# Weight sums of a Strassen-type layer: two groups made anew instead of stored, operand splits ahead of the sink, and the sums of the later products spread over the columns of path A

## The chip, the cores and the metric

The kernel runs on one core of a Trainium2 chip. The metric is the device time of one execution in microseconds; the time before is the median of three runs, and a separate execution was recorded by the hardware profiler. All numbers are float32, multiplied as fp32r (a rounded form that the matrix engine takes) in three passes, high by high, high by low and low by high. TensorE appears as PE (matmuls) and PEld (weight loads), VectorE as DVE, ScalarE as ACT, GpSimd as POOL, SyncE as SP, and SP's queue of transfers as SPq.

## What is computed

One layer of a recurrent mixer over 2048 prompt tokens and 64 sample tokens, with 1024 features. Cut to what matters here:

```python
h = rms_norm(x, g_pre)
vA, bA, cA, zA, q, f, iv, zB, gA, gB = split_cols(h @ w_in)      # ten products, 1024 x 1024 each
conv = causal_conv3([conv_hist, cA * vA], conv_w)
yA = (silu(zA) * bA * conv) @ w_a_out                            # path A
S_new, o = hgrn2_scan(S0, silu(q) * scale, 1 - fg, iv, log(fg))  # path B: 8 heads, chunks of 64 tokens
yB = (rms(o) * g_onorm * silu(zB)) @ w_b_out
merged = sigmoid(gA) * yA + sigmoid(gB) * yB
x = x + rms_norm(merged @ w_o, g_post)
x = x + (p @ w_ple_proj) * sigmoid(rms_norm(x, g_ple) @ w_ple_gate)
```

The kernel names the products `VA, CA, ZA, BA` (path A), `FF0, ZB0, GB...` (path B and the gates), `W_A = w_a_out`, `W_B = w_b_out`, `W_O = w_o` and `W_G = w_ple_gate`.

## The kernel before

**Tiling.** The 2112 tokens are three blocks (0, 1, 2) of 704, features on the partitions. Each matmul takes a 128x128 weight block and half a block of tokens, 352 columns. Weights come from memory in tiles of 128x512 (`raw`, 256 KB, 5 buffers); `split_w` casts each on ACT to `hi` and subtracts on DVE to get `lo`.

**Seven products in place of eight.** `sgroup` (lines 345 to 400) takes two 128-column groups of two products with all 1024 input features as a 2x2 block product and does it with seven half-size products of the Strassen-Winograd kind (lines 380 to 382: high-high, high-low, low-high). This needs four sums of weight quarters, `S1` to `S4` (`total`, line 303), their splits, and sums of the results on DVE (lines 394 to 426: `hf` tiles hold products copied out of the accumulators; the `sink` of each caller writes the outputs). Every product is 12 matmuls, and a group of 7 products 84.

**What is stored.** In block 0, `combined` makes S1 to S4 and the lows of all quarters and stores them in memory (`keep_sum`; `S<-s`, `low<-lo`). Blocks 1 and 2 load sums and lows back (`kept_w`; `raw<-S`, and `s<-low` or `lo<-low`), so that DVE need not make them. The low of a kept quarter goes by turns into an `s` tile (3 of 7; 3 buffers, which the sums use too) or a `lo` tile (`low_tile`). Two groups are not made in block 0, because their products go another way there: the first of head 0 of path B (`FF0`) and the gate columns 6 and 7 (`GB`). `combined` makes their sums when it meets them first, in block 1, and POOL stores sums (line 284) and lows (line 231) for block 2.

**W_A, W_B, W_O and W_G in the same form.** `prepare_sums` makes their sums ahead with loads on POOL's queue (`r<-w_blk`, line 328), sums on DVE (line 358) and stores on POOL (339 sums, 335 lows). It is a generator; hooks between products, or steps of `merge`, call for its next part. `in_turn` (line 486) then goes product by product over all four column groups `g`: at product `n` of group `g` it runs twelve matmuls (lines 513 to 515), the sink (for W_A and W_B: line 419 and line 1171, in the last product, n = 6), and `prepare(i + 1, g)`, which splits the operand of the next product (`operand_of`, DVE line 194). In block 0, W_A and W_B go through `merge` as plain products, and only W_O goes in turn, with its sums made in `merge`.

**Order.** For each block: path B (8 heads, with chunk attention in between), path A (`path_a`, 8 columns j, each a `VA/CA` group, the convolution, and a `ZA/BA` group), W_A, W_B, W_O, the norms, the gates of the next block. Each engine goes through its own list of instructions; the program's order with priorities fixes it. POOL's and SP's transfers are issued in such lists as well, so a transfer that waits holds back those behind it.

Of the kernel before, what the change touches and what calls it, by code (L numbers as in the profile page):

```python
# [20 lines left out]
KB = D // P  # L21
# [67 lines left out]
def hybrid_step(  # L89
# [155 lines left out]
    last, hooks, copies, adds = [None], [], [None], [None]  # L245
# [35 lines left out]
    def keep_sum(name, i1, s, queue):  # L281

        sums.setdefault(i1, {})[name] = dram.tile([P, 4, P], F32, tag=f"{name}_{i1}", name=nm(name), bufs=1)
        queue.dma_start(sums[i1][name], s)
        return split_w(s, (i1, name), queue)
# [8 lines left out]
    def combined(i1, i2, first):  # L294

        queue = SP if first else G
        with tc.high_priority():
            if not first and i1 in sums:
                return {n: kept_w(i1, i2, n) for _, n, _, _, _ in PRODUCTS}
            a11, a21, a22, a12 = (load_raw(w_blk[i, h]) for i, h in ((i1, 0), (i2, 0), (i2, 1), (i1, 1)))  # L300
            out = dict(A11=split_w(a11, (i1, 0), queue))

            def total(name, x, y, op):
                s = sum_tile()
                V.tensor_tensor(s, x, y, op)
                out[name] = keep_sum(name, i1, s, queue)
                return s

            total("S3", a11, a21, ALU.subtract)
            s1 = total("S1", a21, a22, ALU.add)  # L310
            s2 = total("S2", s1, a11, ALU.subtract)
            out["A12"] = split_w(a12, (i1, 1), queue)
            out["A22"] = split_w(a22, (i2, 1), queue)
            total("S4", a12, s2, ALU.subtract)
            return out
# [112 lines left out]
    def plain_group(i1, i2, hs, sink, raws=None, between=None):  # L428


        w, ps = {}, {}

        def split_of(c, h):
            key = ((i1, i2)[c], h)
            raw = raws[c, h] if raws else load_raw(w_blk[key])
            with nullcontext() if raws else tc.high_priority():
                w[c, h] = split_w(raw, key)

        for c, h in ((0, 0), (1, 0)) if between else ((0, 0), (0, 1), (1, 0), (1, 1)):
            with behind_all(() if between else summed[2 + c]):  # L440
                split_of(c, h)

        def add(c, ks):
            for k in ks:
                hi, lo = w[c, k // KH]
                for h in range(2):
                    if (c, h) not in ps:
                        ps[c, h] = ps_gemm()
                    xhi, xlo = hs[k][h]
                    T.matmul(ps[c, h], hi[:, k % KH, :], xhi, start=k == 0, stop=False)  # L450
                    T.matmul(ps[c, h], hi[:, k % KH, :], xlo, start=False, stop=False)
                    last[0] = T.matmul(ps[c, h], lo[:, k % KH, :], xhi, start=False, stop=k == KB - 1).ins

        if between:
            for k in range(KB):
                between()
                for c in range(2):
                    if k == 2:
                        split_of(c, 1)
                    with placed():  # L460
                        add(c, (k,))
        for c in range(2):
            if not between:
                with placed():
                    add(c, range(KB))
            for h in range(2):
                sink(c, h, ps[c, h], None)
# [19 lines left out]
    def in_turn(stages, operand):  # L487


        todo = [(st, n) for st in stages for n in range(7)]  # L490
        made = {0: operand}

        def prepare(i, k):
            if i < len(todo):
                st, n = todo[i]
                made.setdefault(i, []).append(operand_of(st["raw"], IN_TURN[n][1], k))

        for i, (st, n) in enumerate(todo):
            if n == 0:
                st["mid"], st["bank"] = [], {}  # L500
            xs = made.pop(i)
            for g in range(KH):
                i1, i2 = st["idx"] + g, st["idx"] + KH + g
                with tc.high_priority():
                    hi, lo = kept_w(i1, i2, IN_TURN[n][0], IN_TURN[n][0] in st["anew"])
                start = n in (0, 2, 3, 5)
                if start:
                    st["bank"][g] = ps_gemm()
                ps = st["bank"][g]
                add = partial(T.matmul, ps, skip_group_check=not start)  # L510
                for k in range(KH):
                    xhi, xlo = xs[k]
                    add(hi[:, k, :], xhi, start=start and k == 0, stop=False)  # L513
                    add(hi[:, k, :], xlo, start=False, stop=False)  # L514
                    last[0] = add(lo[:, k, :], xhi, start=False, stop=k == KH - 1).ins  # L515
                if n == 0:
                    st["mid"].append(rt())
                    with tc.high_priority():
                        A.copy(half(st["mid"][g], 0), ps)
                u2, p7 = half(st["mid"][g], 0), half(st["mid"][g], 1)  # L520
                if n == 1:
                    st["sink"](g, 0, 0, ps, None)
                elif n == 2:
                    V.tensor_tensor(u2, u2, ps, ALU.add)
                elif n == 3:
                    with tc.high_priority():
                        A.copy(p7, ps)
                elif n == 4:
                    st["sink"](g, 1, 0, u2, ps)
                elif n == 5:  # L530
                    p5 = hf()
                    with tc.high_priority():
                        A.copy(p5, ps)
                    V.tensor_tensor(p7, p7, p5, ALU.add)
                    st["sink"](g, 1, 1, u2, p7)
                elif n == 6:
                    st["sink"](g, 0, 1, u2, ps)
                prepare(i + 1, g)
                hook()
            yield st["idx"], n  # L540

# [585 lines left out]
    def merge(bl, a, kept, extra, ops, ready):  # L1127

        segs = bl["segs"]
        ob, m, mg, loaded = [], [], [], {}  # L1130

        def fetch(kind, j):
            if j < KB:
                loaded[kind, j] = reload(kept[kind, j])

        fetch(GA, 0)
        fetch("o", 0)
        for j, pss in enumerate(gemms(W_A, a, segs)):
            fetch(GA, j + 1)
            fetch("o", j + 1)  # L1140
            if j == KB - 1:
                fetch(GB, 0)
            sg = loaded.pop((GA, j))
            for s, ps in zip(segs, pss):
                V.tensor_tensor(sg[:, cols_of(s)], ps, sg[:, cols_of(s)], ALU.mult)
            m.append(sg)
            ob.append(split_rt(loaded.pop(("o", j))))
            if j:
                next(extra, None)
            if j == KB - 1:  # L1150
                run(ops, 1)
        for j, pss in enumerate(gemms(W_B, ob, segs)):
            fetch(GB, j + 1)
            sg = loaded.pop((GB, j))
            for s, ps in zip(segs, pss):
                V.tensor_tensor(sg[:, cols_of(s)], ps, sg[:, cols_of(s)], ALU.mult)
            V.tensor_tensor(sg, sg, m[j], ALU.add)
            mg.append(sg)
            if j == 0:
                next(extra, None)  # L1160
            if j in (4, 5):
                ready(mg[2 * j - 8 : 2 * j - 6])
            run(ops, (0, 2, 3, 3, 3, 5, 4, 3)[j])
        return mg
# [248 lines left out]
    for bi, bl in enumerate(blocks):  # L1413
# [11 lines left out]
        def side(rows, sums_):  # L1425
            for j in range(KB):
                if 1 <= j <= 4:
                    next(rows, None)
                if j == 3:
                    next(sums_, None)  # L1430
                elif j > 3:
                    hooks.extend(partial(next, sums_, None) for _ in range(5))
                yield

        def ready():
# [26 lines left out]
        else:  # L1462
# [8 lines left out]
            for idx, n in in_turn(stages, a_first):  # L1471
                loads(idx, n)
                if nxt:
                    continue
                if idx == W_O and n in (0, 2, 3, 5):
                    next(again)
                if (idx, n) == (W_O, 4):
                    norms = [final_norm(bl, [s], xo, acc[0], h2, None, True) for s in segs]
                    spread_out((norms[0], (1, 0, 0, 0, 1, 1, 2, 2)))
            if nxt:  # L1480
                assert not hooks
                run(ops)
# [68 lines left out]
```

## Time and profile before

| | |
|---|---|
| median of three runs | 2593.41 us (2591.27 to 2596.1) |
| profiled execution | 2589.74 us, its span 2588.0 us |
| busy in the span | PE 2568.5 us, DVE 1703.2, ACT 1564.0, POOL 395.9 |
| block 0: sums, merge, W_O | up to 832 us |
| gates, final gate, path B of block 1 | 832 to 1283 us |
| path A of block 1 | 1283 to 1509 us |
| W_A, W_B, W_O of block 1 | 1509 to 1675 us |
| path B and path A of block 2 | 1769 to 2058 us and 2058 to 2283 us |
| W_A, W_B, W_O of block 2, then the end with W_G | 2283 to 2448 us, then to 2588 us |

Times in rows of the profile are microseconds from the start of the span. A row of the timeline gives start, duration, engine, line, operation, out<-in, and in brackets the time that the engine sat idle ahead of it and what released it. A PE matmul is shown with the whole of its pipelined time, so the spacing of the starts, not the duration, is what one costs.

### The profile page before, as it was taken

To read this page: it belongs to the slowest core of one execution; us is meant where nothing else is said; L and a number is where in the kernel's file an instruction comes from. 1 tells how busy PE (TensorE), PEld (TensorE's weight loads), DVE (VectorE), ACT (ScalarE), POOL (GpSimd) and SP (SyncE) were. 2 spreads that over 40 slices of the span, in tenths; PEclk is the share of its full clock that TensorE was granted. 3 is DMA by queue.
4 is the path that set the end of the run, shared out by engine and by line. 5 is a ranking of instruction groups with operands and counts; after the bars stand their busy time and mean duration, and the time that the engine had idled before them with its cause. 6 is when DMAs were issued, how large, how long until landed. Compare 5 with 4: busy or idle time off the path is not lost. (4 is left out here: it accounts for less than half of the span.)

```text
span 2588.0 us, 47553 instructions
## 1 busy us (share of the span) xinstructions
PE 2568.5 (99%) x16430; PEld 2554.0 (99%) x16430; DVE 1703.2 (66%) x3354; ACT 1564.0 (60%) x3024; POOL 395.9 (15%) x730
## 2 busy tenths in 40 slices
PE   8999999999999999999999999999999999999999
PEld 8999999999999999999999999999999999999998
DVE  8778888888686455555545579753455544568756
ACT  6666666554436645677745566766677744555736
POOL 2000000110420212211112211021100101210211
PEclk9999999999999999999999999999999999999999
DMA  7787787898878988888889999899777789989977
GB/s 279 250 276 257 256 291 260 310 318 288 323 277 285 388 302 294 281 273 261 257 291 352 383 320 330 288 383 354 229 225 224 224 255 342 391 311 308 348 251 237
DMA packets 370546, 761.73 MB, mean 294 GB/s; under 512 B 45600, under 2 KB 50240, under 8 KB 370304
## 3 DMA queue, kind: packets, MB, share of 16 engines
q1 hardware_dynamic: 326592, 592.13, 67.9%
q0 software_dynamic: 43424, 166.51, 17.3%
q8 instruction: 129, 2.11, 0.4%
q14 instruction: 113, 0.93, 0.1%
q10 hardware_dynamic: 288, 0.05, 0.0%
HBM read 548.52 MB, written 209.99 MB: 293 GB/s over the span
## 5 line engine op out<-in xcount | busy, mean ns | idle before, releaser
L380 PE MATMUL pg<-r,hi 128*128 128x352 f32 x3304 | 1095.7, 332 | 0.8 <-DVE r L426 0.8
L381 PE MATMUL pg<-r,hi 128*128 128x352 f32 x3304 | 1067.9, 323 | 0.0
L224 ACT CAST hi<-raw 128x512 fp32r<-128x512 f32 x760 | 469.1, 619 | 503.0 <-PE pg L381 159.9
L382 PE MATMUL pg<-r,lo 128*128 128x352 f32 x2356 | 762.0, 323 | 2.9 <-DMA lo<-low 2.9
L380 PEld LDWEIGHTS pg<-r,hi 128*128 128x128 f32 x3304 | 622.5, 188 | 2.4 <-issue 1.4
L381 PEld LDWEIGHTS pg<-r,hi 128*128 128x128 f32 x3304 | 623.2, 189 | 0.0
L382 PEld LDWEIGHTS pg<-r,lo 128*128 128x128 f32 x2356 | 443.1, 188 | 3.8 <-DMA lo<-low 3.8
L382 PE MATMUL pg<-r,s 128*128 128x352 f32 x948 | 306.2, 323 | 0.1
L514 PE MATMUL pg<-r,hi 128*128 128x352 f32 x896 | 290.8, 326 | 1.2 <-DVE r L194 0.9
L513 PE MATMUL pg<-r,hi 128*128 128x352 f32 x896 | 286.8, 325 | 0.0
L194 DVE TENSOR_TENSOR r<-r,r 128x352 fp32r<-128x352 f32 (+3 forms) x358 | 215.1, 625 | 53.8 <-ACT r L194 51.8
L194 ACT CAST r<-r 128x352 fp32r<-128x352 f32 (+3 forms) x358 | 190.0, 569 | 45.5 <-DVE r L721 12.5
L194 ACT CAST hi<-raw 128x512 fp32r<-128x512 f32 x202 | 124.8, 620 | 147.9 <-PE pg L381 57.8
L515 PE MATMUL pg<-r,lo 128*128 128x352 f32 x568 | 183.2, 323 | 0.0
L382 PEld LDWEIGHTS pg<-r,s 128*128 128x128 f32 x948 | 178.1, 188 | 0.4 <-DMA s<-low 0.4
L514 PEld LDWEIGHTS pg<-r,hi 128*128 128x128 f32 x896 | 168.7, 188 | 5.4 <-DVE r L194 4.7
L194 DVE TENSOR_TENSOR lo<-raw,hi 128x512 fp32r<-128x512 f32 x202 | 138.3, 686 | 47.6 <-PE pg L548 21.3
L513 PEld LDWEIGHTS pg<-r,hi 128*128 128x128 f32 x896 | 167.6, 188 | 1.7 <-ACT r L194 1.1
L547 PE MATMUL pg<-r,hi 128*128 128x352 f32 x512 | 165.8, 324 | 0.0
L546 PE MATMUL pg<-r,hi 128*128 128x352 f32 x512 | 165.8, 325 | 0.0
L394 ACT COPY hf<-pg 128x352 f32<-128x352 f32 x354 | 156.3, 445 | 2.5 <-PE pg L382 1.8
L194 ACT CAST hi<-s 128x512 fp32r<-128x512 f32 x160 | 98.1, 618 | 98.7 <-PE pg L381 71.4
(376 smaller groups left out, 4126.2 us busy)
## 6 DMA issues: line engine op xcount, KB each, us to landing
raw<-w_blk SPq DMA_DIRECT2D x562, 256.0 KB, 4.3
raw<-S SPq DMA_DIRECT2D x440, 256.0 KB, 4.6
lo<-low SPq DMA_DIRECT2D x434, 256.0 KB, 4.5
s<-low SPq DMA_DIRECT2D x326, 256.0 KB, 4.6
low<-lo SPq DMA_DIRECT2D x298, 256.0 KB, 3.6
S<-s SPq DMA_DIRECT2D x152, 256.0 KB, 3.2
low<-r POOLq DMA_DIRECT2D x68, 256.0 KB, 6.0
r<-w_blk POOLq DMA_DIRECT2D x64, 256.0 KB, 6.8
```

The lines of the kernel that those rows point to most:

```text
L194: return A.copy(hi, src).ins, V.tensor_tensor(lo, src, hi.bitcast(F32), ALU.subtract).ins
L224: A.copy(hi, raw)
L380: add(hi[:, k, :], xhi, start=start and k == 0, stop=False)
L381: add(hi[:, k, :], xlo, start=False, stop=False)
L382: last[0] = add(lo[:, k, :], xhi, start=False, stop=k == KH - 1).ins
L394: copied = A.copy(got[n], ps[bank])
L513: add(hi[:, k, :], xhi, start=start and k == 0, stop=False)
L514: add(hi[:, k, :], xlo, start=False, stop=False)
L515: last[0] = add(lo[:, k, :], xhi, start=False, stop=k == KH - 1).ins
L546: T.matmul(ps, hi[:, k % 4, :], xhi[:, c], start=k == ks[0], stop=False)
L547: T.matmul(ps, hi[:, k % 4, :], xlo[:, c], start=False, stop=False)
```

## The change

Five edits: (1) `combined` stores no sums and lows after block 0, so that the two groups without stored sums are made anew in block 2 as they are in block 1; `plain_group` no longer stores one low that only those would read. (2) In `in_turn` the operand split for the next product stands ahead of the sink where n is 6. (3) In `merge` the steps of W_O's sums come with columns 0 to 7 of W_A instead of 1 to 7 of W_A and 0 of W_B. (4) The sums of W_B (block 1) and W_G (block 2) in path A: a first step at j = 0 and then two or three steps in the hooks of each column, four in the last, instead of one step at j = 3 and five in each of the last four columns. (5) One part of a norm comes one hook later. From line 516 on the changed kernel's lines are shown 2 or 3 higher than before, those of `merge_in_turn` (1171 among them) under the same number.

```diff
@@ combined
             def total(name, x, y, op):
                 s = sum_tile()
                 V.tensor_tensor(s, x, y, op)
-                out[name] = keep_sum(name, i1, s, queue)
+                out[name] = keep_sum(name, i1, s, queue) if first else split_w(s)
                 return s
@@ plain_group
-                w[c, h] = split_w(raw, key)
+                w[c, h] = split_w(raw, None if (c, h) == (1, 0) else key)
@@ in_turn
                     last[0] = add(lo[:, k, :], xhi, start=False, stop=k == KH - 1).ins
+                if n == 6:
+                    prepare(i + 1, g)
                 if n == 0:
...
                 elif n == 6:
                     st["sink"](g, 0, 1, u2, ps)
-                prepare(i + 1, g)
+                if n < 6:
+                    prepare(i + 1, g)
                 hook()
@@ merge
             ob.append(split_rt(loaded.pop(("o", j))))
-            if j:
-                next(extra, None)
+            next(extra, None)
...
             mg.append(sg)
-            if j == 0:
-                next(extra, None)
             if j in (4, 5):
@@ side, in the main loop (runs beside path_a)
                 if 1 <= j <= 4:
                     next(rows, None)
-                if j == 3:
+                if j == 0:
                     next(sums_, None)
-                elif j > 3:
-                    hooks.extend(partial(next, sums_, None) for _ in range(5))
+                else:
+                    at = (2, 9) if j % 2 else (2, 9, 10)
+                    at = (2, 4, 9, 11) if j == KB - 1 else at
+                    hooks.extend(partial(next, sums_, None) if n in at else None for n in range(12))
                 yield
@@ end of block 2
-                    spread_out((norms[0], (1, 0, 0, 0, 1, 1, 2, 2)))
+                    spread_out((norms[0], (0, 1, 0, 0, 1, 1, 2, 2)))
```

With the first edit the stores `S<-s` of line 284 and `low<-lo` of line 231 that stood in POOL's list ahead of and in head 0 of block 1, eight of each (four sums and their lows for each of the two groups), are gone.

**Merge, DVE in block 0.** The first rows are from before, where W_B's columns begin; line 705 scales two tiles of the next block's `x`, line 1156 reads W_B's accumulators, `lo` rows are weight splits.

```order
L358 TENSOR_TENSOR r_9360<-r_9360,r_9357 128x512
L194 TENSOR_TENSOR r_9632<-r_9359,r_9632 128x512
L194 TENSOR_TENSOR r_9648<-r_9357,r_9648 128x512
L194 TENSOR_TENSOR s_9656<-r_9360,s_9656 128x512
L705 SCALAR_TENSOR_TENSOR r_9495<-r_9495,vec,r_9484 128x704
L194 TENSOR_TENSOR lo_9676<-raw_9673,hi_9675 128x512
L705 SCALAR_TENSOR_TENSOR r_9497<-r_9497,vec,r_9484 128x704
L1156 TENSOR_TENSOR r_9461<-pg_9523,r_9461 128x352
L194 TENSOR_TENSOR lo_9750<-raw_9747,hi_9749 128x512
L1156 TENSOR_TENSOR r_9461<-pg_9524,r_9461 128x352
L194 TENSOR_TENSOR lo_9756<-raw_9753,hi_9755 128x512
```

The same place in the changed kernel, where lines 705 and 1156 are 708 and 1158:

```order
L358 TENSOR_TENSOR r_9282<-r_9282,r_9279 128x512
L194 TENSOR_TENSOR r_9500<-r_9279,r_9500 128x512
L194 TENSOR_TENSOR s_9508<-r_9282,s_9508 128x512
L194 TENSOR_TENSOR lo_9672<-raw_9669,hi_9671 128x512
L1158 TENSOR_TENSOR r_9472<-pg_9551,r_9472 128x352
L194 TENSOR_TENSOR lo_9746<-raw_9743,hi_9745 128x512
L1158 TENSOR_TENSOR r_9472<-pg_9552,r_9472 128x352
L194 TENSOR_TENSOR lo_9752<-raw_9749,hi_9751 128x512
L1159 TENSOR_TENSOR r_9472<-r_9472,r_8714 128x704
L708 SCALAR_TENSOR_TENSOR r_9523<-r_9523,vec,r_9512 128x704
L708 SCALAR_TENSOR_TENSOR r_9525<-r_9525,vec,r_9512 128x704
```

The three weight splits stood behind the first row of line 705 and now stand ahead of it.

**From W_A to W_B, DVE in block 1.** Before; `lo` rows are weight splits, rows of line 194 that write `r` are operand splits for W_B's first product, 419 and 1171 the sink of W_A's last:

```order
L194 TENSOR_TENSOR r_19946<-r_19697,r_19946 128x352
L419 TENSOR_TENSOR hf_19967<-r_19321,pg_19839 128x352
L194 TENSOR_TENSOR lo_20080<-raw_20077,hi_20079 128x512
L1171 TENSOR_TENSOR r_19257<-hf_19967,r_19257 128x352
L194 TENSOR_TENSOR r_19970<-r_19699,r_19970 128x352
L194 TENSOR_TENSOR lo_20104<-raw_20101,hi_20103 128x512
L419 TENSOR_TENSOR hf_19991<-r_19345,pg_19867 128x352
L194 TENSOR_TENSOR r_19994<-r_19701,r_19994 128x352
L1171 TENSOR_TENSOR r_19259<-hf_19991,r_19259 128x352
L419 TENSOR_TENSOR hf_20015<-r_19369,pg_19895 128x352
L194 TENSOR_TENSOR r_20018<-r_19703,r_20018 128x352
L1171 TENSOR_TENSOR r_19261<-hf_20015,r_19261 128x352
```

In the changed kernel (1171 is shown under the same number, the splits follow each other closer):

```order
L194 TENSOR_TENSOR r_19907<-r_19661,r_19907 128x352
L194 TENSOR_TENSOR r_19931<-r_19663,r_19931 128x352
L194 TENSOR_TENSOR lo_20044<-raw_20041,hi_20043 128x512
L419 TENSOR_TENSOR hf_19934<-r_19285,pg_19803 128x352
L194 TENSOR_TENSOR r_19955<-r_19665,r_19955 128x352
L194 TENSOR_TENSOR lo_20068<-raw_20065,hi_20067 128x512
L1171 TENSOR_TENSOR r_19221<-hf_19934,r_19221 128x352
L419 TENSOR_TENSOR hf_19958<-r_19309,pg_19831 128x352
L194 TENSOR_TENSOR r_19979<-r_19667,r_19979 128x352
L1171 TENSOR_TENSOR r_19223<-hf_19958,r_19223 128x352
```

The four operand splits (19946, 19970, 19994, 20018 before; 19907, 19931, 19955, 19979 now) had three, two and two other rows between them; now none, two and three. The splits of the second to fourth column group stood behind the row of line 419 of their group and stand ahead of it now.

**Path A, DVE in block 1.** Before: the four sums (line 358) at one of their four places, among the rows with which a group ends (405, 400, 426):

```order
L405 TENSOR_TENSOR hf_17950<-hf_17950,hf_17973 128x352
L358 TENSOR_TENSOR r_18019<-r_18018,r_18019 128x512
L400 TENSOR_TENSOR hf_17927<-hf_17927,pg_17983 128x352
L358 TENSOR_TENSOR r_18018<-r_18017,r_18018 128x512
L426 TENSOR_TENSOR r_17867<-hf_17927,hf_17950 128x352
L358 TENSOR_TENSOR r_18017<-r_18019,r_18017 128x512
L358 TENSOR_TENSOR r_18020<-r_18020,r_18017 128x512
L426 TENSOR_TENSOR r_17867<-hf_17927,pg_17937 128x352
L816 TENSOR_TENSOR r_17868<-pg_17914,r_17867 128x352
```

In the changed kernel, at the matching place:

```order
L405 TENSOR_TENSOR hf_18125<-hf_18125,hf_18140 128x352
L400 TENSOR_TENSOR hf_18110<-hf_18110,pg_18150 128x352
L358 TENSOR_TENSOR r_18166<-r_18165,r_18166 128x512
L358 TENSOR_TENSOR r_18165<-r_18164,r_18165 128x512
L358 TENSOR_TENSOR r_18164<-r_18166,r_18164 128x512
L426 TENSOR_TENSOR r_18054<-hf_18110,hf_18125 128x352
L358 TENSOR_TENSOR r_18167<-r_18167,r_18164 128x512
L426 TENSOR_TENSOR r_18054<-hf_18110,pg_18112 128x352
L851 TENSOR_TENSOR r_17889<-r_17889,r_18054 128x704
```

The sums have moved from a `VA/CA` group (its next rows are the convolution's, line 816) to the `ZA/BA` group of the column before (next row line 851), and stand in front of both rows of line 426 as they did. The first of the four sets has moved out of path A into the attention rows of the last head of path B.

## The prediction

> **What bounds the kernel.** I read the page first, then PE's waits, then the timeline at each wait, and last what the releasing engine did just before.
>
> The page's first part, then who PE waited for (total us, times, longest):
>
> ```profile
> PE 2568.5 (99%) x16430; PEld 2554.0 (99%) x16430; DVE 1703.2 (66%) x3354; ACT 1564.0 (60%) x3024; POOL 395.9 (15%) x730
> PE pg L382 <- DMA lo<-low: 2.9, 3, 2.0
> PE pg L514 <- DVE r L194: 0.9, 2, 0.7
> PE pg L548 <- DVE lo L194: 0.9, 1, 0.9
> PE pg L380 <- DVE r L426: 0.8, 2, 0.6
> ```
>
> PE is busy 99% and the change takes no matmul away, so only PE's waits can go; the four rows shown belong to four different edits. Idle time in these rows understates a wait, because a matmul's end is modelled; I therefore count starts. Where nothing waits, a 352-column matmul starts every 0.16 us, as 1564.85 to 1565.01 below shows.
>
> **Edit 1, stores of two groups (block 1, head 0).** PE's timeline, the stretch with the clock (busy, count, granted clock, DMA share, GB/s), then SP's waits from 985 to 1035 us and POOL's and SP's issues:
>
> ```profile
> 1005.73 0.32 PE L381 MATMUL pg<-r,hi 128*128 128x352 f32 x1
> 1006.76 0.43 PE L382 MATMUL pg<-r,lo 128*128 128x352 f32 x1 [0.71 <-DMA lo<-low]
> 1029.91 0.32 PE L381 MATMUL pg<-r,hi 128*128 128x352 f32 x1
> 1032.18 0.43 PE L382 MATMUL pg<-r,lo 128*128 128x352 f32 x1 [1.96 <-DMA lo<-low]
> ...
> 1032.15:1036.35 4.20, 4.17 (x16) 0.59 0.97 342
> ...
> SPq L225 <- DMA S<-s: 11.8, 4, 4.7
> ...
> 1024.35 0.54 POOL L284 DMA_DIRECT2D S<-s  x1
> ...
> 1025.45 0.45 SPq L225 DMA_DIRECT2D lo<-low  x1
> 1030.70 0.32 SPq L225 DMA_DIRECT2D s<-low  x1
> ```
>
> PE lost 1006.76 - 1005.73 - 0.16 = 0.87 us at the first wait and 1032.18 - 1029.91 - 0.16 = 2.11 at the second. Afterwards 16 matmuls took 4.20 us where 16 x 0.16 = 2.56 would do, 1.64 more, at a granted clock of 0.59. Together 4.6 us. The loads were late because SP's list was held: a low goes into an `s` buffer, the three `s` buffers were held by sums until POOL's store of them had landed, and SP waited 11.8 us for that in four times, once between 1025.45 and 1030.70 for the store issued at 1024.35. Everything behind in SP's list waited too. Without the stores a sum's buffer comes free after its DVE and ACT split, which stand right behind it, and 16 transfers of 256 KB are gone from the same stretch. SP's four waits are four times as long as PE's two (2.98 us), so I take the whole 4.6 as gained; if another hold of `s` takes the place of the stores, about half, 2.3.
>
> The Trainium skill ("TensorE: Matmul & The Clock Gate", section "What's actually happening") has the clock halved after an idle window of about 3.4 us, with windows that run freely. The trace shows it halved after 2.11 us already, and not after 0.87. By that rule the half clock need not come in every execution, which would leave 4.6 - 1.6 = 3.0 us of gain here; the sum below goes by the trace.
>
> What edit 1 adds lies in block 2, where the two groups' sums and lows are made anew: 8 sums and 8 splits on DVE in place of loads. The trace has the price of one in block 1, and of the stretch that gets them (span, then PE, PEld, DVE, ACT, POOL busy, clock, DMA share, GB/s):
>
> ```profile
> L305 DVE TENSOR_TENSOR s<-raw,raw 128x512 f32<-128x512 f32 x80 | 54.7, 684 | 4.9 <-DMA raw<-w_blk 2.9 <-PE pg L382 1.7 <-DMA S<-s 0.2
> 1769.00:1815.00 46.00, 46.00 (x288) 46.00 (x287) 17.18 (x33) 31.29 (x53) 3.72 (x8) 1.00 0.95 334
> ```
>
> 16 x 0.68 = 11 us of DVE, in a stretch where DVE is busy 17.2 of 46 us. It then is busy 28, as PE needs each split only 12 matmuls, 1.9 us, after the last, and sums wait for four quarters instead of one. I price it at 0: cover is DVE's idle half, and SP's list, which loses 14 loads over the two groups (four quarters and three lows each in place of seven tiles and seven lows). Bounds: -0.4 (a DMA share of 0.95 falls) and, if sums are late, what the first wait of block 1 cost, 0.87 + 0.1, for either group, +1.9.
>
> **Edit 2, operand splits ahead of the sink (block 1, W_A to W_B).** PE and DVE:
>
> ```profile
> 1564.23 0.32 PE L513 MATMUL pg<-r,hi 128*128 128x352 f32 x1
> 1564.58 0.43 PE L514 MATMUL pg<-r,hi 128*128 128x352 f32 x1
> 1564.85 0.33 PE L515 MATMUL pg<-r,lo 128*128 128x352 f32 x1
> 1565.01 0.32 PE L513 MATMUL pg<-r,hi 128*128 128x352 f32 x1
> 1566.05 0.43 PE L514 MATMUL pg<-r,hi 128*128 128x352 f32 x1 [0.72 <-DVE r L194]
> 1566.80 0.33 PE L514 MATMUL pg<-r,hi 128*128 128x352 f32 x1
> 1567.35 0.43 PE L514 MATMUL pg<-r,hi 128*128 128x352 f32 x1 [0.23 <-DVE r L194]
> ...
> 1565.05 0.51 DVE L419 TENSOR_TENSOR hf<-r,pg 128x352 f32<-128x352 f32 x1
> 1565.48 0.51 DVE L194 TENSOR_TENSOR r<-r,r 128x352 fp32r<-128x352 f32 x1
> 1565.92 0.51 DVE L1171 TENSOR_TENSOR r<-hf,r 128x352 f32<-128x352 f32 x1
> ```
>
> Gaps of 0.19, 0.88 and 0.39 us, plus 0.11 after each (1564.58 to 1564.85 is 0.27): 1.8 us. Each time PE waits for an operand's low that stands behind sink rows in DVE's list, at 0.43 us a row (1565.05 to 1565.48). In the new order the second and third split have three sink or weight rows (0.43 to 0.6 us each) fewer ahead of them, and the fourth two; that is about 1.5, 1.5 and 0.9 us earlier, more than each gap. What is late next is the weight `lo` that the splits now precede, and the first split, which hasn't moved: I take 1.3 of 1.8 (0.5 to 1.8). The other transitions and block 2 show no such gap: 0.
>
> **Edit 3, W_O's sums a column earlier (block 0).** PE, DVE and POOL:
>
> ```profile
> 731.22 0.32 PE L547 MATMUL pg<-r,hi 128*128 128x352 f32 x1
> 732.41 0.43 PE L548 MATMUL pg<-r,lo 128*128 128x352 f32 x1 [0.87 <-DVE lo L194]
> ...
> 730.80 0.95 DVE L705 SCALAR_TENSOR_TENSOR r<-r,vec,r 128x704 f32<-128x704 f32 x1 [5.85 <-DMA r<-x_fm]
> 731.67 0.68 DVE L194 TENSOR_TENSOR lo<-raw,hi 128x512 fp32r<-128x512 f32 x1
> ...
> 722.15 1.14 POOL L655 DMA_DIRECT2D r<-x_fm  x2
> ```
>
> DVE stood 5.85 us on `x`, and the weight low behind it let PE wait 732.41 - 731.22 - 0.16 = 1.03 us (and 0.1 after). In the new order that low and the next two stand ahead of the `x` rows. The `x` loads stand behind eight more of POOL's issues (0.54 us each) and land later by up to 4.3 us, at 735; the rows then behind DVE's wait free an accumulator that PE needs only two columns on. So -1.1; from -1.2 to +1 (the same wait, moved). DVE's W_A stage gets one more step of sums in place of W_B's: 0.
>
> **Edit 4, sums spread over path A.** PE at its two waits in block 1, DVE there, DVE's waits from 1283 to 1509 us, POOL's loads ahead of the first, and the page's row of all such loads:
>
> ```profile
> 1416.42 0.32 PE L382 MATMUL pg<-r,s 128*128 128x352 f32 x1
> 1417.36 0.40 PE L380 MATMUL pg<-r,hi 128*128 128x352 f32 x1 [0.62 <-DVE r L426]
> 1444.32 0.32 PE L382 MATMUL pg<-r,s 128*128 128x352 f32 x1
> 1444.84 0.40 PE L380 MATMUL pg<-r,hi 128*128 128x352 f32 x1 [0.20 <-DVE r L426]
> ...
> 1413.23 0.69 DVE L358 TENSOR_TENSOR r<-r,r 128x512 f32<-128x512 f32 x1 [6.64 <-DMA r<-w_blk]
> 1416.70 0.52 DVE L426 TENSOR_TENSOR r<-hf,pg 128x352 f32<-128x352 f32 x1
> ...
> DVE r L358 <- DMA r<-w_blk: 26.1, 4, 8.0
> ...
> 1403.36 1.60 POOL L328 DMA_DIRECT2D r<-w_blk  x3
> ...
> r<-w_blk POOLq DMA_DIRECT2D x64, 256.0 KB, 6.8
> ```
>
> PE lost 0.78 and 0.36 us, and 0.07 after each: 1.3 us. The four sums wait for POOL's loads and stand in front of the two rows of line 426 that free an accumulator. In the new order they stand in front of the same two rows, once in each of columns 2, 4 and 6, in the other group of the column (the set before these goes to the attention). So the wait isn't removed, it is moved. By the row of POOL and the first sum at 1413.23 a load took some 9 us; the median of all 64 is 6.8. The group takes 84 x 0.16 = 13.4 us; I estimate from the order that the last load of a set is now issued 5.4 us into its group, so that the sums start 12 to 15 us in, and that PE waits from 14 on, half a microsecond later than before, since the first row of line 426 has only one accumulator's ACT step ahead. Two of three events are then free: I take 0.8 gained of 1.3. Ends: -1.3, and +2 if every event costs what 1417 did and the set in the attention waits too. In block 2 the same four waits cost PE nothing before: 0, up to +1.
>
> **Edit 5**, a norm's step a hook later, costs nothing: PE does not wait there.
>
> **Sum.** -4.6 - 1.3 - 1.1 - 0.8 = -7.8 us on the profiled execution of 2589.74, so 2581.9. That execution was 3.7 us faster than the median of 2593.41; taking the difference over, the median is 2585.6 us. I call no change what lies within 0.2%, 5.2 us, about what a measurement of this kernel can tell.
>
> **Rivals.**
>
> 1. *The spread sums wait more than they did.* For it: DVE's waits for such loads already come to 26.1 us in four. Each of the six events in columns 2, 4 and 6 of two blocks then costs the 0.85 of the one at 1417, +5.1 in place of -0.8: -7.0 + 5.1 = -1.9, 2591.5. Against it: in block 2 waits of that kind cost nothing. The Trainium skill ("DMA: Bandwidth & Descriptors", section "Queues, rings and completion order") has every engine take turns between queues packet by packet, so POOL's loads slow SP's and the other way round, which speaks for this rival; the bytes in path A, though, stay the same. Chance 0.2.
> 2. *Another hold of the `s` buffers.* SP then waits for a split or a low in use, and edit 1 gives 2.3: -5.5, 2587.9. Chance 0.12.
> 3. *No half clock in most executions.* Edit 1 gives 3.0: -6.2, 2587.2. Chance 0.08.
> 4. *Slower.* One late set of sums per event grows to over 2 us and brings the half clock with it, as at 1032: 2.2 + 1.6 = 3.8 us each, six times 23, less the gain of 7.0: +16, 2609. It decides from 2.0 us per event on (six events need 12.2 to reach slower by 0.2%). Against it: the longest such wait of DVE, 8.0 us, cost PE 0.85. Chance 0.07.
>
> **Chances and range.** The forecast has 0.53. Faster by over 0.2%: forecast 0.51, rival 2 0.07, rival 3 0.06, so 0.64. Within 0.2%: the rest of these and 0.18 of rival 1, 0.27. Slower: 0.09. The range goes from all gains in full (4.6 + 0.4 + 1.8 + 1.2 + 1.3 = 9.3, and 3 us, most of the 3.7 by which the profiled execution was faster) at 2581 to rival 1 with 1 us an event, 2592.5.
>
> **What would show it.** Right: SP's waits for `S<-s` are absent after 985 us and PE starts matmuls every 0.16 us through 1005 to 1036; three gaps at the start of W_B of block 1 are under 0.3 us; line 548 no longer waits for a weight low in W_B of block 0; waits of line 380 on line 426 total under 0.8. Wrong: waits on line 426 in both blocks (rival 1), SP held for an `s` buffer by other rows (rival 2), line 382 or 380 waiting for DVE's splits at 1769 to 1815, where block 2 makes its sums anew.

## The result and the profile after

The changed kernel takes 2597.12 us (median of 20 runs, 2592.92 to 2603.01) against 2592.34 us (median of 20, 2586.7 to 2596.1). The ratio is 1.0019 with a 95% interval of 1.0013 to 1.0026: slower by 0.19%, where 0.30% faster was forecast; that is just inside what the prediction called no change, but the interval holds no gain. The profiled execution has a span of 2593.7 us, 5.7 more than before.

The page's first part and PE's waits (total, times, longest):

```profile
PE 2568.2 (99%) x16430; PEld 2554.4 (98%) x16430; DVE 1713.0 (66%) x3370; ACT 1564.5 (60%) x3024; POOL 391.2 (15%) x714
PE pg L382 <- DMA lo<-low: 3.2, 2, 2.6
PE pa L963 <- DVE att L987: 3.0, 1, 3.0
PE pa L965 <- DVE att L987: 2.4, 1, 2.4
PE pg L551 <- DVE lo L194: 1.2, 1, 1.2
PE pg L514 <- DVE r L194: 1.0, 1, 1.0
PE pg L549 <- DVE r L1148: 0.9, 1, 0.9
```

The line 426 is gone from the list, as forecast, and two waits on the attention (`att`) are new. Both programs give PE the same 16430 matmuls, so the starts of the same matmul can be subtracted. What the changed kernel gained or lost in each stage, with two more columns for runs told below (us, against the first profile of before, the one on which the prediction rests):

| stage | changed | edit 5 alone | before, second profile |
|---|---|---|---|
| merge, block 0 | +2.5 | -0.3 | +0.2 |
| path B head 0, block 1 | -4.8 | -2.5 | -1.0 |
| last head, block 1 | +4.7 | 0.0 | 0.0 |
| path A, block 1 | -1.2 | -0.3 | +0.1 |
| W_B, block 1 | -0.1 | -1.2 | -1.2 |
| path B head 0, block 2 | +4.4 | 0.0 | 0.0 |
| last head, block 2 | +2.6 | 0.0 | 0.0 |
| last norm, 2432 to 2496 us | -0.9 | -0.9 | +4.4 |
| all else | -1.5 | -1.0 | -1.1 |
| sum | +5.7 | -6.1 | +1.3 |

Edit 5 touches only the last norm, and the last column is the kernel before itself; still both differ by 1 to 2.5 us in stages whose code is unchanged. So a figure of about 1 us in one profile is not yet an edit's effect; how far each stage varies is given with the single edits.

**Head 0 of block 1** is as forecast: SP's waits on `S<-s` are gone, and PE ran without a gap (span, PE busy, PEld, DVE, ACT, POOL, clock, DMA share, GB/s):

```profile
1000.00:1036.00 36.00, 36.00 (x226) 35.98 (x225) 19.37 (x38) 25.27 (x43) 2.29 (x5) 1.00 0.79 265
```

**Head 0 of block 2** lost what block 1 gained. DVE, SP with its largest wait, PE, then the stretches in which SP stood, caught up, and PE ran again:

```profile
1765.75 0.53 DVE L405 TENSOR_TENSOR hf<-hf,hf 128x352 f32<-128x352 f32 x1 [5.92 <-ACT hf L394]
1766.79 0.69 DVE L305 TENSOR_TENSOR s<-raw,raw 128x512 f32<-128x512 f32 x1 [0.52 <-PE pg L382]
1770.16 0.69 DVE L305 TENSOR_TENSOR s<-raw,raw 128x512 f32<-128x512 f32 x1
...
1761.54 2.28 SPq L204 DMA_DIRECT2D raw<-w_blk  x2
1770.88 1.40 SPq L204 DMA_DIRECT2D raw<-S  x2
SPq L204 <- DVE s L305: 7.7, 2, 7.0
...
1785.15 0.43 PE L382 MATMUL pg<-r,lo 128*128 128x352 f32 x1 [2.63 <-DMA lo<-low]
...
1763.00:1771.00 8.00, 8.00 (x52) 8.00 (x51) 4.73 (x8) 2.92 (x7) 1.00 (x2) 1.00 0.78 298
1780.00:1785.00 5.00, 2.51 (x16) 2.22 (x14) 1.05 (x2) 1.60 (x3) 0.00 (x0) 1.00 1.03 398
1786.00:1789.00 3.00, 3.00 (x12) 3.00 (x11) 0.52 (x1) 0.62 (x1) 0.00 (x0) 0.50 0.44 163
```

The four quarters hold four of five `raw` tiles until the sums are made. The sums stand in DVE's list behind the row of line 405, which waited 5.92 us for the copy of its group's product, and SP's next load went out when the second sum ended, at 1770.85, with other rows of DVE between the two sums. So SP could issue no load for 7.0 us, the kept lows behind it included. Then the DMA engines ran full (share 1.03) and did not catch up; PE waited 2.8 us and went on at half clock. This chain is read from the trace; no run below removes it by itself.

**The attention of the last head** has the first set of sums now. POOL, DVE and PE in block 1, with the stretch behind:

```profile
1272.08 1.12 POOL L328 DMA_DIRECT2D r<-w_blk  x2
1280.61 0.54 POOL L1061 DMA_DIRECT2D o<-r  x1 [7.41 <-DVE r L1048]
1281.15 1.06 POOL L328 DMA_DIRECT2D r<-w_blk  x2
...
1288.80 0.69 DVE L358 TENSOR_TENSOR r<-r,r 128x512 f32<-128x512 f32 x1 [4.61 <-DMA r<-w_blk]
1290.61 0.29 DVE L987 COPY_PREDICATED att<-caus,pa 128x128 f32<-128x128 int32 x1
...
1290.96 0.42 PE L963 MATMUL pa<-ident,r 128*128 128x128 f32 x1 [2.98 <-DVE att L987]
...
1291.60:1294.50 2.90, 2.90 (x12) 2.90 (x12) 2.07 (x4) 0.28 (x2) 1.62 (x3) 0.50 0.94 352
```

Two of the four loads stand in POOL's list behind a store that waited 7.41 us for DVE. They landed at 1288.8; DVE's first sum waited for them in front of the attention's row of line 987, and PE waited for that row 3.1 us, then ran a dozen matmuls at half clock. Block 2 has the same place, 2.5 us of wait at 2074, with no half clock behind it.

**Merge.** DVE's gate row, POOL's reload ahead of it, the `x` row, and PE's three waits:

```profile
717.90 0.54 POOL L339 DMA_DIRECT2D S<-r  x1
718.43 0.54 POOL L335 DMA_DIRECT2D low<-s  x1
718.96 0.54 POOL L1125 DMA_DIRECT2D r<-g__934_3754  x1
...
723.93 0.96 DVE L1148 TENSOR_TENSOR r<-pg,r 128x352 f32<-128x352 f32 x2 [5.77 <-DMA r<-g__934_3754]
739.67 0.95 DVE L708 SCALAR_TENSOR_TENSOR r<-r,vec,r 128x704 f32<-128x704 f32 x1 [3.27 <-DMA r<-x_fm]
...
716.42 0.43 PE L550 MATMUL pg<-r,hi 128*128 128x352 f32 x1 [0.78 <-DVE r L194]
724.51 0.43 PE L549 MATMUL pg<-r,hi 128*128 128x352 f32 x1 [0.91 <-DVE r L1148]
733.59 0.43 PE L551 MATMUL pg<-r,lo 128*128 128x352 f32 x1 [1.23 <-DVE lo L194]
```

DVE no longer stands on `x` ahead of the weight lows; the wait on `x` costs PE nothing. The wait on a weight low at the start of W_B stayed all the same (733.59). DVE stood 5.77 us on the gate of W_A's last column, whose reload (`r<-g`) stands in POOL's list behind the stores of a set of sums, and those wait for DVE; the sums that it made up for afterwards stood ahead of that weight low.

**W_A to W_B.** PE and the last operand split:

```profile
1565.23 0.32 PE L513 MATMUL pg<-r,hi 128*128 128x352 f32 x1
1566.59 0.43 PE L514 MATMUL pg<-r,hi 128*128 128x352 f32 x1 [1.03 <-DVE r L194]
...
1566.02 0.52 DVE L194 TENSOR_TENSOR r<-r,r 128x352 fp32r<-128x352 f32 x1
```

Three waits have become one of 1.2 us (and one of 0.3 us at 1575). The first product of W_B needs all four operands within its first twelve matmuls, and the fourth split ends at 1566.5, where before it ended at 1567.3.

### The profile page after: what moved, and what is told of

Read it like the earlier page. It is cut to its first block, busy times and chain, and to the rows that moved or that the text cites. A ratio compares the mean times of both kernels' runs of the same rounds, so it can differ in the third digit from the quotient of the medians.

```text
span 2593.7 us, 47519 instructions
## 1 busy us (share of the span) xinstructions
PE 2568.2 (99%) x16430; PEld 2554.4 (98%) x16430; DVE 1713.0 (66%) x3370; ACT 1564.5 (60%) x3024; POOL 391.2 (15%) x714
## 3 DMA queue, kind: packets, MB, share of 16 engines
q8 instruction: 129, 2.11, 0.3%
## 4 chain that ended last, share of the span: by engine, by line
PE 93%; DMA 3%; DVE 2%; issue 1%; ACT 1%; POOL 0%; SPq 0%; DVEq 0%; ACTq 0%; POOLq 0%
PE pg L380 20%; PE pg L382 20%; PE pg L381 20%; PE pg L514 5%; PE pg L513 5%; PE pg L515 5%; PE pg L551 2%; PE pg L549 2%; PE pg L550 2%; PE pa L996 1%; PE pa L1032 1%; PE pa L1034 1%; DMA lo<-low 1%; PE pa L982 1%; PE pa L1104 1%
```

## The experiments

The theory after the first reading: each edit does alone what the stage table shows, by the lists just named. The rival: the new waits come of shifts that the edits bring about together.

**Single edits.** `keep_only` is before with edit 1, `merge_only` with edit 3, `spread_only` with edit 4. `spread_pin1` is edit 4 with the first set pinned:

```diff
+        def pinned(sums_):
+            with tc.issue_after(adds[0]):      # on DVE: not before the last product's sum
+                next(sums_, None)
-  hooks.extend(partial(next, sums_, None) if n in at else None for n in range(12))
+  hooks.extend(partial(pinned if j < 3 else step, sums_) if n in at else None for n in range(12))
```

> Edit 1 alone (no stores of the two groups' sums and lows after block 0, so both are made anew in block 2). Theory: the edit has two sides that the changed kernel's trace shows, about -4.7 us at 1005 to 1036 and about +4.4 us at the head of path B of block 2 (a PE wait of 2.8 us near 1781 and a dozen matmuls at half clock behind it), because SP's list stands for 7 us on weight buffers that the sums of line 305 still hold; the time is then that of before within 1 us, and both places are seen in this trace. Rival: the wait in block 2 comes from the other edits' shifts, and edit 1 alone gains its 4.7 us: 0.18% faster.

> Edit 3 alone (W_O's sums one column earlier in merge). Theory: slower by 2 to 2.5 us between 700 and 757 us: PE waits near 716, 724 and 733 of 0.9 to 1.4 us each, since the reload of the gate of the last W_A column stands in POOL's list behind stores that wait for DVE's sums. Rival: the three waits belong to the changed timing ahead of the merge, and this kernel shows the 1.1 us gain that was forecast.

> Edit 4 alone (sums of W_B and W_G spread over path A). Theory: +4.7 us near 1288 (block 1) and +2.6 near 2072 (block 2), where the first set of sums stands among the attention rows of the last head, and -1.3 us at 1417 and 1445: about 6 us slower, 0.23%. Rival: the waits near 1288 and 2072 come of loads that the other edits slowed, and the spread alone gains about 1 us.

> Edit 4 alone, but on DVE the first set's four sums are queued behind the product in whose hook they are called (columns 1 and 2), so that they leave the attention; the other three sets stand where edit 4 has them, and POOL's loads are unchanged. Theory: the waits near 1288 and 2072 vanish and the gain of 1.3 us at 1417 and 1445 stays: 1 to 1.5 us faster than before. Rival: what makes PE wait in the attention is the set's loads or stores and not the sums' place in DVE's list; then the waits stay, about 6 us slower.

Against the first profile of before, in the stages of the table:

| kernel | ratio (95%) | its own stages |
|---|---|---|
| keep_only | 0.9996 (0.9985 to 1.0007) | head 0 block 1 -4.3, head 0 block 2 +1.8 |
| merge_only | 1.0016 (1.0004 to 1.0028) | merge +2.5 |
| spread_only | 1.0040 (1.0026 to 1.0055) | last heads +4.4 and +2.6, path A -0.9 |
| spread_pin1 | 1.0008 (0.9999 to 1.0016) | last heads 0.0 and +0.1, path A -1.3 |

The theory holds for place and sign: every loss appears with its edit alone. With four rows of DVE moved and POOL's loads as they were, both waits in the attention vanish, so the sums' place is the cause there. In spread_pin1 POOL's loads go out as late as before, the attention's row no longer waits for them, and the sums come behind the group's end:

```profile
1284.57 0.54 POOL L1058 DMA_DIRECT2D o<-r  x1 [7.44 <-DVE r L1045]
1285.11 1.06 POOL L328 DMA_DIRECT2D r<-w_blk  x2
...
1289.99 0.30 DVE L984 COPY_PREDICATED att<-caus,pa 128x128 f32<-128x128 int32 x1 [0.41 <-PE pa L979]
1311.58 0.68 DVE L358 TENSOR_TENSOR r<-r,r 128x512 f32<-128x512 f32 x1
```

The size at the head of block 2 varies (1.8 us here, with no half clock). And the stages vary without any edit. In profiles of kernels that leave a stage's code alone, the last heads and the head of block 2 stay within 0.1 us of the first profile, but head 0 of block 1 lies at -2.5 to +0.3 (seven profiles), path A of block 1 at -1.4 to +0.1 (nine), merge at -1.1 to +1.6 (nine) and W_B of block 1 at -1.2 to +1.9 (twelve). So edit 1's gain in block 1 and all the losses stand clear of this, and the gain of about 1 us in path A does not.

The times fit the traces less well: spread_pin1 is not the 1 to 1.5 us faster that was expected, and spread_only loses 10 us (0.40%) where its own stages show 6. One stage that none of these edits touches differs in all four: the last norm, where keep_only, merge_only, spread_only and spread_pin1 show +3.5, +6.4, +3.1 and +4.0. That asked for the next two.

**Edit 5 alone and before again.**

```diff
-                    spread_out((norms[0], (1, 0, 0, 0, 1, 1, 2, 2)))
+                    spread_out((norms[0], (0, 1, 0, 0, 1, 1, 2, 2)))
```

> Edit 5 alone (a norm's step one hook later near the end). Theory: PE's wait at 2452 us, 0.9 us in the profile of before, 2.5 to 3.9 in those of the single edits and absent in the changed kernel, is set by this edit: it is absent here, and the kernel is 1 to 3 us faster than before. Rival: that wait differs from execution to execution with the pace of weight loads, and edit 5 does nothing: it is seen here too, and the time is that of before.

> The kernel before, profiled once more. Theory: PE's wait at 2452 us (0.9 us in the first profile, 2.5 to 3.9 in seven of the kernels without edit 5) differs from execution to execution, and the first profile showed a short one; here it is 2 to 4 us. Rival: it is 0.9 again, and the single edits lengthened it.

Edit 5 alone is faster: 0.9984 (0.9973 to 0.9994). The second profile of before shows PE's wait at 2452 us at full size; ACT's row is the cast ahead of the step that DVE waits for:

```profile
PE pa L631 <- DVE r L651: 3.5, 1, 3.5
...
2448.05 0.62 ACT L224 CAST hi<-raw 128x512 fp32r<-128x512 f32 x1 [3.08 <-DMA raw<-w_blk]
2449.10 0.53 DVE L651 TENSOR_TENSOR r<-r,hf 128x352 f32<-128x352 f32 x1 [3.68 <-ACT hf L650]
```

A cast of a late weight tile stands in ACT's list ahead of a norm's step. Ten of the eleven profiles without edit 5 lose 2.4 to 4.1 us there; the first of before, on which the prediction rests, lost 0.9. The five with it lose under 0.4. The order changes by a handful of rows (a transposition on PE, two on ACT, four on DVE); which of them gives the loads their lead was not tried.

**Where the gain and loss of edit 1 come from.** `own_tiles` and `own_both` keep the 16 stores, but make the sums (`own_both`: the lows too) in ring tiles, so that stores hold no `s` (and no `lo`) tile; `keep_ring` is edit 1 with the four quarters loaded into ring tiles.

```diff
own_tiles, own_both, in total():
-                s = sum_tile()
+                s = sum_tile() if first else ring_tile()
own_both also, in split_w():
-        lo = wp.tile([P, 4, P], F32R, tag="lo", name=nm("lo"))
+        lo = wp.tile([P, 4, P], F32R, tag="lo", name=nm("lo")) if queue is SP else ring_tile(F32R)
keep_ring, in combined():
-            a11, a21, a22, a12 = (load_raw(w_blk[i, h]) for ...)
+            load = load_raw if first else load_ring        # SP.dma_start into a ring tile
```

> Before, with one change: in block 1 the sums of the two groups are made in ring tiles of their own instead of the three s tiles; all sums and lows are stored as before, and block 2 loads them. Theory: what cost PE 4.7 us at 1005 to 1036 was that loads of lows waited for s tiles held by stores, not the stores' share of the DMA engines, so 4 to 4.7 us go there and nothing is paid in block 2: about 0.17% faster. Rival: the 16 stores' traffic makes the loads late; then at most 1 us goes.

> Before, but in block 1 both the sums and the lows of the two groups are made in ring tiles of their own and stored from there, so that neither s nor lo tiles are held by a store; all 16 stores stay. Theory (holds): SP's waits on stores are gone and PE loses under 1 us between 1000 and 1040 us. Rival (traffic): the DMA engines are full there, the 16 stores delay the loads, and PE still loses 2 us or more without any wait of SP on a store.

> Edit 1 alone, but the four quarters of the two groups are loaded into ring tiles instead of the five raw tiles, in blocks 1 and 2. Theory: PE waits at the head of block 2 because the quarters hold raw tiles until the sums of line 305 are made, and SP's list, kept low loads included, stands behind the next load into a raw tile; with raw tiles free the wait of 1.8 us (edit 1 alone) falls below 0.4, and the gain in block 1 stays: about 1.8 us faster than edit 1 alone. Rival: the loads are late because the sums and lows themselves are late on DVE; then the wait of 1.8 us stays.

own_tiles missed: 1.0000 (0.9991 to 1.0008), head 0 of block 1 +0.2. SP's waits from 985 to 1035 us show why, first own_tiles, then own_both:

```profile
SPq L225 <- DMA low<-lo: 5.8, 3, 3.7
```

```profile
SPq L228 <- PE pg L551: 12.5, 4, 5.4
SPq L228 <- PE pg L385: 11.9, 11, 1.6
```

With the `s` tiles free, the `lo` tiles were held by their stores, and PE lost 2.3 us at 1008 with the half clock behind it. (SP's longest waits there, 15.6 us in four, were for `raw` tiles whose sums were not yet made.) With both free, SP waits for no store and head 0 of block 1 gains 3.2 us, with one PE wait of 0.9 us left, although the DMA engines are as full as before where PE waited first (share 1.03 from 1000 to 1010 us, 1.01 in the first profile of before; columns as above):

```profile
1000.00:1010.00 10.00, 10.00 (x64) 10.00 (x63) 5.29 (x10) 4.36 (x9) 3.37 (x7) 1.00 1.03 408
```

So it was the held tiles, both kinds, and not the traffic. The 3.2 us lie only 0.7 beyond the -2.5 that the stage shows in edit 5 alone, where nothing there was changed; best_stored below, with the same tiles, gains 4.0. The whole own_both comes out at 0.9999 (0.9987 to 1.0010), not the gain that its stage alone would give: merge, whose code it leaves alone, shows +1.6 us, and there is a wait of 2.4 us at 2452.

keep_ring also missed, 1.0039 (1.0024 to 1.0054): head 0 shows +3.2 us in block 1 and +4.1 in block 2. Its longest group of PE's waits in the whole run, and SP's from 1760 to 1790 us:

```profile
PE pg L386 <- ACT hi L229: 6.9, 4, 1.9
...
SPq L230 <- DVE lo L194: 11.8, 2, 10.6
```

The quarters' loads went out from 1767.85 us on, in the changed kernel by 1763.8; why they came later was not tried. PE waited for the cast of a late quarter (`hi`), and SP stood 10.6 us for an `s` tile instead of 7.0 for a `raw` tile. The run shows neither theory right; one held kind of tile took the place of another.

**Merge.** `merge_ahead` is edit 3 with the gate asked for a column earlier.

```diff
         fetch("o", 0)
+        fetch(GA, 1)
         for j, pss in enumerate(gemms(W_A, a, segs)):
-            fetch(GA, j + 1)
+            fetch(GA, j + 2)
```

> Edit 3 alone, and the gate tile of each W_A column is asked for one column earlier, so that the last one stands in POOL's list ahead of the stores of the sums. Theory: of the 2.5 us that edit 3 loses between 700 and 757 us, the waits near 716 to 724 (over 1.3 us) go, and the wait near 733 goes or stays by itself; 1.3 to 2.5 us less than edit 3 alone. Rival: DVE's own load in the W_A columns makes the waits; then they stay.

DVE's rows for the last gate of W_A then stand without a wait:

```profile
711.26 0.52 DVE L1146 TENSOR_TENSOR r<-pg,r 128x352 f32<-128x352 f32 x1
713.21 0.52 DVE L1146 TENSOR_TENSOR r<-pg,r 128x352 f32<-128x352 f32 x1
```

The stage goes from +2.5 to -1.2 with no PE wait over 0.3 us left in it; 0.9997 (0.9987 to 1.0008) as a whole. The reload's place in POOL's list was the cause of the loss. Whether edit 3 then brings the 1.1 us that were forecast is less certain: all four profiles with it and the earlier reload show -1.2, but of the nine without edit 3, which lie from -1.1 to +1.6, two show no wait there either.

**Edit 2, and the sum.** `split_only` is edit 2 alone. `best_nosplit` has edits 1, 3, 4 and 5 with the two mends, `best_all` edit 2 as well, and `best_stored` is best_nosplit with own_both's tiles and stores in place of edit 1.

> Edit 2 alone. Theory: the fourth operand split, which moved up by 0.8 us only, sets PE's wait, and rows that the splits now precede are late elsewhere; the start of W_B in block 1 changes by less than 0.5 us and the time by nothing that can be told. Rival: the forecast gain of 1.3 us between 1556 and 1606 us.

> All five edits, with two mends: the first set of sums in path A queued behind its hook's product on DVE, and the gate tiles in merge asked for a column earlier. Theory: the edits' effects add up: about -1 in merge, -3 to -4.5 at the head of block 1, -1.2 in path A, nothing in the attention, -2.5 to -4 at 2452, against +2 to +4 at the head of block 2: about 7 us or 0.27% faster than before. Rival: waits move on (as they did in three runs) and the sum is within 0.2%.

> The same without edit 2 (operand splits behind the sink, as before). Theory: edit 2 moves PE's waits at the start of W_B of block 1 but the last of the four splits still sets their sum, so this is within 1 us of the run with it, and PE loses 1 to 1.8 us there in both. Rival: edit 2 gains the 1.3 us that were forecast; then this one is 1.3 us slower.

> Edits 3, 4 and 5 with their two mends, no edit 2, and in place of edit 1 the two groups' sums and lows made in ring tiles in block 1 and stored from there, so that block 2 loads them. Theory: no PE wait at the head of block 2 (2.2 us in the same kernel with edit 1), about 3 us gained at the head of block 1, so 9 to 10 us or 0.37% faster than before. Rival: the wait at the head of block 2 comes with the timing of the rest, and is seen here too; then it is no faster than the same kernel with edit 1.

| kernel | ratio (95%) | median us | head 0, blocks 1 and 2 |
|---|---|---|---|
| split_only | 1.0000 (0.9991 to 1.0009) | 2591.67 | +0.2, -0.1 |
| best_all | 0.9969 (0.9957 to 0.9981) | 2584.08 | -4.8, +2.1 |
| best_nosplit | 0.9963 (0.9951 to 0.9975) | 2582.10 | -4.8, +2.2 |
| best_stored | 0.9969 (0.9956 to 0.9981) | 2584.74 | -4.0, +0.1 |

Three versions beat the kernel before by 0.3 to 0.4%, and so the changed one too; their intervals overlap, and the 0.27% expected of best_all lies within its own. best_stored has no PE wait at the head of block 2, as the stretch there shows (PE busy all of its 45 us): the wait comes with making the sums anew, not with the timing of the rest. Yet it is not faster than best_nosplit, where its theory had 3 us.

```profile
1755.00:1800.00 45.00, 45.00 (x281) 45.00 (x280) 17.63 (x32) 28.73 (x50) 3.22 (x6) 1.00 0.96 351
```

Edit 2 shows no gain: in split_only W_B of block 1 is 1.2 us shorter than in the first profile of before, and so it is in the second profile of before and with edit 5 alone, where nothing there was changed; best_all loses 1.2 us more in W_A than best_nosplit.

## Why the prediction was wrong

The forecast was -7.8 us on the profiled execution, and it moved by +5.7. Three steps failed, and together they cost 15.3 us against the forecast, more than the 13.5 between the two: the set of sums in the attention, which the sum took at nothing (7.3), the cover for the sums made anew in block 2 (4.4), and POOL's order in merge (3.6).

- **Edit 1, block 1** (-4.6): right, -4.8, and for the reason given, except that the `lo` tiles are part of it. The gain is that large only against the first profile: the second lost 1.0 us less there, and edit 5 alone, with the stores in place, 2.5 less.
- **Edit 1, block 2** (0, at most +1.9): wrong, +4.4, and 1.8 to 2.2 in three other kernels with the edit. The step that failed is the cover. I counted DVE's idle half and the loads that go; DVE was in fact idle, but its list put the sums behind a row that waited, and by the trace what was scarce was `raw` tiles on SP's list in a stretch whose DMA share, 0.95, stood in the row quoted. That the sums made anew bring the wait is shown (keep_only, best_stored); that the `raw` tiles do is not, since keep_ring freed them and waited for others. "Sums wait for four quarters instead of one" was written and not followed to SP.
- **Edit 2** (-1.3): about 0. By the trace the fourth split, which moves least, sets the end; and the 1.8 us were one execution's.
- **Edit 3** (-1.1): +2.5. The order on DVE was read rightly, POOL's only for the `x` loads; the reloads of the gates behind the moved stores were missed. With the reloads moved the stage shows -1.2.
- **Edit 4, columns** (-0.8): -1.2, near the forecast, but in part by luck: path A is up to 1.4 us shorter in kernels without the edit, and in keep_only and own_tiles the two waits of line 380 are absent too. **Edit 4, attention** ("the set in the attention waits too", within +2): +4.7 and +2.6. The cost was taken from the rows of line 426; but the rows behind the sums are now the attention's, on which PE waits at once, and block 2 was priced from four waits that stand elsewhere.
- **Edit 5** (0, "PE does not wait there"): the wait on line 651 was in the very list quoted, with 0.7 us, and left out. In ten other profiles without the edit it is 2.4 to 4.1 us, in nine of them with the half clock behind it.
- **Profile and median.** The difference of 3.7 us was carried over as if it had no place. One place is known: the second profile is 4.4 us longer in the last norm. It is shorter elsewhere and only 1.3 us longer as a whole, so the rest stays open.
- **Rivals.** The slow one came near: late sums that cost PE over 2 us each, but in the attention, at two places and not six, and only the one at 1290 brought the half clock, for 1.6 us (as the wait at 1785 did, which is edit 1's). Rival 1's waits on line 426 did not come. Rival 3 was half right: of the eight profiles that leave the stores and tiles of head 0 of block 1 as they were, four show the half clock there and four do not. No rival had the head of block 2, though the signs of being wrong named that place, or the reloads in merge.

## What to carry to other kernels

When PE is the bound and 0.2% is the question, follow each moved step down every list on which it stands, transfers first: who is behind it, which tiles it holds, and whether the DMA engines have room to catch up. A scheduler may hoist a spread step out of the stage that it was meant for, so read the neighbours in the order, not the hook. And take a wait's size from two executions before pricing its removal: in the kernel before, one wait was 0.9 us in the first profile and 3.7 in the second, and gains of about 1 us in path A, W_B and merge appeared in profiles where nothing there had been changed.

## What the runs showed of the hardware

PE's half clock follows a wait irregularly. In the 16 profiles of this case, apart from the start and the end, the granted clock fell to 0.50 for 3.41 us at a time, twice for 6.83 us; measured on the starts of the same matmuls in a profile without it, such a stretch behind a wait of 2 us or more cost 1.5 to 1.7 us, the long ones 2.4 and 2.7. Taking a wait as the distance of two starts less 0.16 us, all nine waits of 2.78 us or more were followed by it. Between 2.0 and 2.7 us it went both ways: eight waits brought it, 2.11 us (before) and 2.37 (split_only) among them, and seven did not, such as 2.18 (best_all) and 2.58 (own_both). Below 2.0 us it came only twice, in keep_ring, after two waits close together (1.81 and 1.82 us, 1.01 and 0.88). So the price of a wait near 2 us jumps by some 1.6 us from one place or execution to the next. The Trainium skill ("TensorE: Matmul & The Clock Gate", section "What's actually happening") states an idle window of about 3.4 us; the length of the stretches agrees with it, but these runs show the half clock after waits well below it.
